# The MLP's seven-product scheme with its token halves exchanged, and VectorE and ScalarE in program order during the output projection

## The chip, the cores and the metric

The kernel runs on one core of one Trainium2 chip. Its time is the device time of one execution in microseconds; of several runs the median is taken. The engines are named as the profile names them: PE (matmul, with PEld for its weight loads), DVE (VectorE), ACT (ScalarE), POOL (GpSimd) and SP (SyncE, which here issues DMAs).

## The reference

One block of a decoder for 512 tokens and 1024 dimensions: a norm, an input projection, two kinds of sparse attention, a gated merge of the two, an output projection with a residual add, and an MLP. The change touches what comes from the output projection on:

```python
    mix = (jax.nn.sigmoid(gate_a) * (o_a @ w_branch_a[l])
           + jax.nn.sigmoid(gate_b) * (o_b @ w_branch_b[l]))
    x = x + mix @ w_out[l]                       # 512x1024 @ 1024x1024
    h = rmsnorm(x, norm_mlp[l])
    x = x + jnp.square(jax.nn.relu(h @ w_mlp_in[l])) @ w_mlp_out[l]   # 1024 -> 4096 -> 1024
return rmsnorm(x, norm_final)
```

## The kernel before

All products are float32 made of three float32r matmuls: a factor is cast to a high part (on ACT), the difference to it is its low part (a subtraction on DVE or POOL), and high*high, high*low and low*high are added up in PSUM.

**Output projection.** The merged branches lie in SBUF as mixh and mixl, 128 dimensions by 512 tokens in 8 chunks, made in the order 4, 5, 6, 7, 0, 1, 2, 3. The result is made in 8 tiles of 128 tokens by 512 dimensions: wo00 to wo03 for the first half of the dimensions, wo10 to wo13 for the second. A tile is 24 matmuls: 16 that go through the chunks with mixh and mixl against wo0hh (the high part of w_out), then 8 with wo0hl. The weights of the second half (wo1r, loaded in 8 pieces, then wo1hh and wo1hl) are split while the first half is running. Behind each tile DVE adds it to the residual x2, ACT makes its sum of squares (sq, with ssq) and, in the first half, a root of the mean (rt); DVE takes the reciprocal (rti) and makes xg, the tile times that preliminary factor and times the norm's weights. PE transposes xg in four matmuls (L1401), placed among the matmuls of the following tile: `TP` says after how many.

**The MLP's first layer** takes its channels in 16 pairs of blocks (2 x 128). A pair is a product of two by two blocks (halves of the dimensions by halves of the tokens, and halves of the dimensions by the two channel blocks), made in seven block products instead of eight, numbered 1 to 7. Each has an operand of x2 (a token half of a dimension half, or a sum or difference of two: `x_sum`, the xt tiles; split by `x_split` into xb, xd or xshh and xshl) and an operand of weights (`w_part`: the sum ws if one is needed, its high part wm on ACT and its low part on POOL, or on DVE for the products of `LOV` from pair 2 on). The loads are wmi, one pair in two tiles. A product is 12 matmuls of 256 tokens into a PSUM tile z. `collect` copies it (ACT) or adds it (DVE) to one or two halves of zt, as `uses` has it. ORDER is the order of the products. Of pair 0 four products belong to the output projection's block of code, with six weight operands made ahead of them (the list `w0`).

**The second layer** (mo) follows in groups of four channel blocks; its weights wmoh and wmol come from wmor, and the result is added to x2 by DVE with the rows' final norm factor r2, which `row_factors` makes from ssq and rt: five small operations on 4 elements a row.

**What sets the order.** A scheduler orders each engine's instructions from the program's, except inside a `manual_schedule`, where the named engines keep program order. Before, such a block covers PE alone, and begins at the transposes in tile wo10; it ends behind the first four products. Tiles come from pools by tag with a fixed number of buffers (`ta` five, `m` two, `q` four, `wr` three): a new tile waits for the last reader of the one whose buffer it takes. DMA loads stand on SP's queue in order.

## Time and profile before

| | us |
|---|---|
| median of 3 runs | 788.96 |
| lowest and highest | 786.49, 788.99 |
| profiled execution, its run's time | 791.72 |
| profiled execution, its span | 789.9 |
| of it: everything before the output projection | 387.1 |
| output projection, to the first product of the MLP | 48.9 |
| MLP's pairs 0 to 3, with two token tiles of the second layer's first group | 58.7 |
| from there to the last group of the second layer | 257.3 |
| last group and final norm | 37.9 |

The stages' bounds are first matmuls in the trace (387.11, 436.02, 494.75, and the last group at about 752). Times inside the profiled execution add up to its span, and not to a median. A row of the timeline has the start, the length, engine, line, operation, what is written and read, shape and count; in brackets the idle time of the engine just before it and what ended it. An engine's instructions overlap by a little, so the pace is the distance of two starts and not the length of one.

### The profile page before, as it was taken

To read this page: it belongs to the slowest core of one execution; us is meant where nothing else is said; L and a number is where in the kernel's file an instruction comes from. 1 tells how busy PE (TensorE), PEld (TensorE's weight loads), DVE (VectorE), ACT (ScalarE), POOL (GpSimd) and SP (SyncE) were. 2 spreads that over 40 slices of the span, in tenths; PEclk is the share of its full clock that TensorE was granted. 3 is DMA by queue.
4 is the path that set the end of the run, shared out by engine and by line. 5 is a ranking of instruction groups with operands and counts; after the bars stand their busy time and mean duration, and the time that the engine had idled before them with its cause. 6 is when DMAs were issued, how large, how long until landed. Compare 5 with 4: busy or idle time off the path is not lost.

```text
span 789.9 us, 12161 instructions
## 1 busy us (share of the span) xinstructions
PE 752.7 (95%) x4267; PEld 645.9 (82%) x4267; DVE 578.7 (73%) x1301; ACT 470.8 (60%) x975; POOL 290.4 (37%) x183
## 2 busy tenths in 40 slices
PE   7999898999999999989999979999999999999996
PEld 4888687777887788867877979888888999999985
DVE  5344678999999966656747999778778696877444
ACT  6533786778667889985344755645454454644234
POOL 3714643232332347763122862312223141414022
PEclk9999999999999999999999999999999999999999
DMA  9454736253344425464630623222314141413002
GB/s 293 112 165 136 202 88 164 80 141 93 94 140 117 153 69 169 140 229 163 237 107 15 225 81 107 80 89 76 130 54 160 54 160 54 161 54 107 1 27 108
DMA packets 87502, 95.55 MB, mean 121 GB/s; under 512 B 8598, under 2 KB 69654, under 8 KB 87408
## 3 DMA queue, kind: packets, MB, share of 16 engines
q1 hardware_dynamic: 83984, 92.97, 36.9%
q0 software_dynamic: 3456, 1.80, 1.2%
q8 instruction: 34, 0.56, 0.3%
q14 instruction: 28, 0.23, 0.1%
HBM read 86.29 MB, written 14.74 MB: 128 GB/s over the span
## 4 chain that ended last, share of the span: by engine, by line
PE 66%; DVE 19%; ACT 6%; DMA 5%; issue 2%; POOL 1%; SPq 0%; DVEq 0%; ACTq 0%; POOLq 0%
PE mo L1551 8%; PE mo L1554 7%; PE mo L1552 7%; PE z L117 6%; PE z L113 6%; PE z L114 6%; PE wo L1438 2%; PE pg L125 2%; PE pg L123 2%; DVE work L667 2%; PE pg L128 2%; DVE ws L1330 2%; DVE m L666 2%; DVE work L648 1%; DMA w1rv<-in_cmp_w_v 1%
## 5 line engine op out<-in xcount | busy, mean ns | idle before, releaser
L1552 PE MATMUL mo<-wmoh,al 128*128 128x512 f32 (+1 forms) x260 | 100.6, 390 | 0.6 <-DVE al L1494 0.6
L1551 PE MATMUL mo<-wmoh,ah 128*128 128x512 f32 (+1 forms) x260 | 100.9, 393 | 0.3 <-ACT ah L1492 0.2
L1503 POOL TENSOR_TENSOR wmol<-wmor,wmoh 128x1024 fp32r<-128x1024 f32 x17 | 49.6, 2921 | 114.1 <-ACT wmoh L1502 114.0
L1334 POOL TENSOR_TENSOR wm<-wmi,wm 128x512 fp32r<-128x512 f32 x32 | 50.1, 1583 | 109.5 <-ACT wm L1333 109.5
L1333 ACT CAST wm<-ws 128x512 fp32r<-128x512 f32 x80 | 49.3, 622 | 49.4 <-PE z L117 25.3
L1555 DVE SCALAR_TENSOR_TENSOR x<-mo,r,x 128x512 f32<-128x512 f32 (+1 forms) x65 | 47.7, 739 | 41.2 <-PE mo L1554 41.0
L1554 PE MATMUL mo<-wmol,ah 128*128 128x512 f32 (+1 forms) x260 | 70.3, 392 | 0.0
L106 POOL TENSOR_TENSOR wg_l<-wr_g,wg_h 128x1024 fp32r<-128x1024 f32 x16 | 38.4, 2401 | 80.2 <-PE pg L128 29.6
L113 PE MATMUL z<-xshh,wm 128*128 128x256 f32 x256 | 64.1, 283 | 2.5 <-DVE zt L1350 2.5
L1350 DVE TENSOR_TENSOR zt<-zt,z 128x256 f32<-128x256 f32 x128 | 48.6, 413 | 23.4 <-ACT zt L1348 16.8
L114 PE MATMUL z<-xshl,wm 128*128 128x256 f32 x256 | 63.9, 282 | 0.0
L1330 DVE TENSOR_TENSOR ws<-wmi 128x512 f32<-128x512 f32 x74 | 62.3, 852 | 1.0 <-POOL wm L1334 0.7
L1348 ACT ACTIVATE zt<-z 128x256 f32<-128x256 f32 x64 | 22.5, 384 | 65.8 <-PE z L117 65.8
L1551 PEld LDWEIGHTS mo<-wmoh,ah 128*128 128x128 f32 x260 | 48.7, 188 | 11.7 <-DVE x L1555 0.6
L1334 DVE TENSOR_TENSOR wm<-ws,wm 128x512 fp32r<-128x512 f32 x70 | 52.3, 763 | 8.2 <-ACT wm L1333 8.2
L1552 PEld LDWEIGHTS mo<-wmoh,al 128*128 128x128 f32 x260 | 48.9, 188 | 11.2 <-DVE al L1494 0.8
L1554 PEld LDWEIGHTS mo<-wmol,ah 128*128 128x128 f32 x260 | 48.6, 188 | 11.0
L1502 ACT CAST wmoh<-wmor 128x1024 fp32r<-128x1024 f32 x32 | 32.1, 1050 | 41.5 <-PE mo L1552 35.1
L123 PE MATMUL pg<-hTh,wg_h 128*128 128x512 f32 x128 | 53.0, 414 | 0.0
L125 PE MATMUL pg<-hTl,wg_h 128*128 128x512 f32 x128 | 52.6, 411 | 0.0
L113 PEld LDWEIGHTS z<-xshh,wm 128*128 128x128 f32 x256 | 48.7, 190 | 2.9 <-issue 1.7
L114 PEld LDWEIGHTS z<-xshl,wm 128*128 128x128 f32 x256 | 48.7, 190 | 0.0
(427 smaller groups left out, 2206.3 us busy)
## 6 DMA issues: line engine op xcount, KB each, us to landing
wmi<-in_w_mlp_in SPq DMA_DIRECT2D x32, 512.0 KB, 4.8
wmor<-in_w_mlp_out SPq DMA_DIRECT2D x32, 512.0 KB, 3.6
wr_g<-in_w_in SPq DMA_DIRECT2D x16, 512.0 KB, 3.8
d_rev<-d_vr SPq DMA_DIRECT2D x8, 640.0 KB, 5.7
x<-in_x SPq DMA_DIRECT2D x8, 512.0 KB, 7.8
d_t<-th SPq DMA_DIRECT2D x16, 256.0 KB, 2.0
stb<-d_rev SPq DMA_DIRECT2D x8, 256.0 KB, 2.8
wr_qa<-in_w_in SPq DMA_DIRECT2D x4, 512.0 KB, 3.6
```

The lines of the kernel that those rows point to most:

```text
L113: PE.matmul(o, wh(k), xh(k), start=start and n == 0, stop=False)
L114: PE.matmul(o, wh(k), xl(k), start=False, stop=False)
L123: PE.matmul(o, wh(k), xh(k), start=k == 0, stop=False)
L125: PE.matmul(o, wh(k), xl(k), start=False, stop=False)
L1330: V.tensor_tensor(t, src, more[0], op=w_blocks[m][2])
L1333: A.copy(w[:, 0], src)
L1334: (V if p > 1 and m in LOV else G).tensor_sub(w[:, 1], src, w[:, 0].bitcast(F32))
L1350: V.tensor_tensor(c, c, o, op=ALU.add if sign > 0 else ALU.subtract)
L1503: (V if ff % 4 in LOO and ff else G).tensor_sub(lo, r, hi.bitcast(F32))
L1551: PE.matmul(o, act[f][0][:, js], wm[f][0][:, cs], start=f == 0, stop=False)
L1552: PE.matmul(o, act[f][1][:, js], wm[f][0][:, cs], start=False, stop=False)
L1554: PE.matmul(o, act[f][0][:, js], wm[f][1][:, cs], start=False, stop=f == FG - 1)
```

## The change

Five edits, all between the start of the output projection and the MLP's first pairs.

1. The token halves change places in the scheme: what the products took from the second half they now take from the first, and the other way round. The blocks of x2 are made in the order (0,0), (0,1), (1,0), (1,1): dimension half, token half. Before, product 2 takes (0,0), 6 the sum (0,0)+(0,1), 4 (1,0)-(0,0), and four need the last block: 5 takes (1,1), 1 (0,0)+(1,1), 7 (1,0)+(1,1), 3 (0,1)-(1,1). After, 2 takes (0,1), 6 (0,0)+(0,1), 1 (0,1)+(1,0), 3 (0,0)-(1,0), 5 (1,0), and two need the last block: 4 takes (1,1)-(0,1), 7 (1,0)+(1,1). `uses` is exchanged to match, `ORDER` is 2, 6, 5, 1, 3, 4, 7 instead of 2, 4, 6, 1, 7, 5, 3, and the six weight operands made ahead are now those of 2, 6, 5, 1, 3, 4.
2. PE, DVE and ACT keep program order in the whole output projection, where before PE alone did in its second half. For this the splits of x2's operands, which were generators stepped through by a list (`GO`), are now two parts: `x_split` makes the high parts and returns a function `lo` for the low parts, called behind the next tile's square.
3. In the second half xg is made ahead of the square. Transposes come after 14 matmuls of the next tile instead of 12, 12 and 10.
4. Low parts of weights: those of pair 1 for products 1, 2, 5, 6, 7 run on DVE instead of POOL. Low parts of x2's operands on POOL: those of 3 and 7 in token tiles 0, 1 and 2, 3, where before those of 7 (tile 2) and 3 (tiles 2 and 3).
5. In `row_factors` POOL makes four of the five operations (the reduction becomes an add of two columns), DVE the reciprocal.

```diff
-    ORDER = (2, 4, 6, 1, 7, 5, 3)
+    ORDER = (2, 6, 5, 1, 3, 4, 7)
-    TP = ((18, 18, 18, 18), (18, 12, 12, 10))
-    XP = ((7, 2), (3, 2), (3, 3))
+    TP = ((18, 18, 18, 18), (18, 14, 14, 14))
+    WP = (0, 0, 1, 1, 1, 1, 1, 1)
+    XP = ((3, 0), (3, 1), (7, 2), (7, 3))
-    uses = {3: ((0, 1, 1), (1, 1, 1)), 5: ((0, 1, 1), (0, 0, -1)), 1: ((0, 0, 1), (1, 1, 1)),
-            2: ((1, 1, -1), (1, 0, 1)), 4: ((0, 0, 1), (1, 0, 1)), 6: ((1, 1, 1),), 7: ((0, 0, 1),)}
+    uses = {3: ((0, 0, 1), (1, 0, 1)), 5: ((0, 0, 1), (0, 1, -1)), 1: ((0, 1, 1), (1, 0, 1)),
+            2: ((1, 0, -1), (1, 1, 1)), 4: ((0, 1, 1), (1, 1, 1)), 6: ((1, 0, 1),), 7: ((0, 1, 1),)}
...
-        (V if p > 1 and m in LOV else G).tensor_sub(w[:, 1], src, w[:, 0].bitcast(F32))
+        (V if p and m in LOV else G).tensor_sub(w[:, 1], src, w[:, 0].bitcast(F32))
...
         if q == (0, 0):
-            gens = [x_split(2, j, t)]
+            ops = []
         elif q == (0, 1):
-            gens = [x_sum(6, j, full(0, 0), t, ALU.add)]
+            ops = [x_sum(6, j, full(0, 0), t, ALU.add), (2, j, t)]
         elif q == (1, 0):
-            gens = [x_sum(4, j, t, full(0, 0), ALU.subtract)]
+            ops = [x_sum(1, j, full(0, 1), t, ALU.add), x_sum(3, j, full(0, 0), t, ALU.subtract), (5, j, t)]
         else:
-            gens = [x_split(5, j, t), x_sum(1, j, full(0, 0), t, ALU.add),
-                    x_sum(7, j, full(1, 0), t, ALU.add), x_sum(3, j, full(0, 1), t, ALU.subtract)]
-        for i in GO if len(gens) > 1 else (0,) * 3:
-            next(gens[i], None)
+            ops = [x_sum(4, j, t, full(0, 1), ALU.subtract), x_sum(7, j, full(1, 0), t, ALU.add)]
+        los = [x_split(*o) for o in ops]
+        return lambda: [f() for f in los]
...
+    ms2.enter_context(tc.manual_schedule(engines={eng.PE, eng.DVE, eng.Activation}))
...
-                    if (half, j) == (1, 0):
-                        ms2.enter_context(tc.manual_schedule(engines={eng.PE}))
-                    x2_transposes(*last)
+                    los = x2_transposes(*last)
...
+            if half:
+                V.scalar_tensor_tensor(xg, x2[j][:, cs], rti[:, j:j + 1], gmlp[:, cs], op0=ALU.mult, op1=ALU.mult)
             A.activation(sq, x2[j][:, cs], AF.Square, accum_out=ssq[:, j, half:half + 1])
             if half == 0:
                 A.activation(rt[:, j:j + 1], ssq[:, j, 0:1], AF.Sqrt, bias=eps_t, scale=1.0 / S)
+            if los:
+                los()
+            if half == 0:
                 V.reciprocal(rti[:, j:j + 1], rt[:, j:j + 1])
-            V.scalar_tensor_tensor(xg, x2[j][:, cs], rti[:, j:j + 1], gmlp[:, cs], op0=ALU.mult, op1=ALU.mult)
+                V.scalar_tensor_tensor(xg, x2[j][:, cs], rti[:, j:j + 1], gmlp[:, cs], op0=ALU.mult, op1=ALU.mult)
-            for _ in range((0, 0, 1, 1, 2, 1, 1, 0)[half * NT + j]):
+            for _ in range(WP[half * NT + j]):
...
-        V.tensor_reduce(r2, ssq, axis=AX.X, op=ALU.add)
-        V.tensor_scalar(r2, r2, 1.0 / DM, EPS, op0=ALU.mult, op1=ALU.add)
+        G.tensor_add(r2, ssq[:, :, 0], ssq[:, :, 1])
+        G.tensor_scalar(r2, r2, 1.0 / DM, EPS, op0=ALU.mult, op1=ALU.add)
         V.reciprocal(r2, r2)
-        V.tensor_mul(rt, rt, rt)
-        V.tensor_mul(r2, r2, rt)
+        G.tensor_mul(rt, rt, rt)
+        G.tensor_mul(r2, r2, rt)
```

What moves on the engines, at three places. In the rows a name with its tile number is written, then what is read (numbers behind an underscore are the buffers').

PE, the end of the first tile of the output projection, before:

```order
L1438 MATMUL wo00_4692<-wo0hh_3955,mixh_4452 128x512
L1438 MATMUL wo01_4724<-wo0hh_3955,mixh_4452 128x512
L1438 MATMUL wo02_4767<-wo0hh_3955,mixh_4452 128x512
L1438 MATMUL wo02_4767<-wo0hh_3955,mixl_4453 128x512
L1438 MATMUL wo02_4767<-wo0hh_3955,mixh_4452 128x512
L1438 MATMUL wo00_4692<-wo0hh_3955,mixl_4453 128x512
L1438 MATMUL wo00_4692<-wo0hh_3955,mixh_4452 128x512
L1438 MATMUL wo01_4724<-wo0hh_3955,mixl_4453 128x512
L1438 MATMUL wo00_4692<-wo0hh_3955,mixl_4453 128x512
L1438 MATMUL wo00_4692<-wo0hl_3956,mixh_4452 128x512 x8
```

and after, the end of wo00 and the start of wo01, and further on in wo01 the transposes of xg00, which stand before the last six of its 24 matmuls:

```order
L1439 MATMUL wo00_4694<-wo0hh_3955,mixh_4452 128x512
L1439 MATMUL wo00_4694<-wo0hh_3955,mixl_4453 128x512
L1439 MATMUL wo00_4694<-wo0hl_3956,mixh_4452 128x512 x8
L1439 MATMUL wo01_4726<-wo0hh_3955,mixh_4452 128x512
L1439 MATMUL wo01_4726<-wo0hh_3955,mixl_4453 128x512
```

```order
L1439 MATMUL wo01_4726<-wo0hh_3955,mixh_4452 128x512
L1439 MATMUL wo01_4726<-wo0hh_3955,mixl_4453 128x512
L1439 MATMUL wo01_4726<-wo0hl_3956,mixh_4452 128x512 x2
L1404 MATMUL xt00_4745<-ident_76,xg00_4720 128x128 x4
L1439 MATMUL wo01_4726<-wo0hl_3956,mixh_4452 128x512 x6
L1439 MATMUL wo02_4765<-wo0hh_3955,mixh_4452 128x512
```

The first three tiles' matmuls, which were taken in turn, are now one tile after the other.

ACT, the splits of wo1r's last pieces and the square of the first tile, before:

```order
L475 CAST wo1hh_4646<-wo1r6_4672 128x512
L475 CAST wo1hh_4646<-wo1r7_4676 128x512
L1333 CAST wm0_4_4857<-wmi01_4681 128x512
L1441 ACTIVATE sq00_4718,ssq_4688<-x2_0_4634 128x512
L1443 ACTIVATE rt_4690<-ssq_4688,small_75 128x1
```

after:

```order
L475 CAST wo1hh_4646<-wo1r6_4672 128x512
L1445 ACTIVATE sq00_4721,ssq_4688<-x2_0_4634 128x512
L475 CAST wo1hh_4646<-wo1r7_4676 128x512
L1447 ACTIVATE rt_4690<-ssq_4688,small_75 128x1
L1412 COPY xf00_4750<-xt00_4745 128x4x128
```

and DVE behind it, where xg00 and so the first transposes come from, before:

```order
L476 TENSOR_TENSOR wo1hl_4647<-wo1r6_4672,wo1hh_4646 128x512
L1439 SCALAR_TENSOR_TENSOR x2_0_4634<-wo00_4692,x2_0_4634 128x512
L1444 RECIPROCAL rti_4691<-rt_4690 128x1
L1439 SCALAR_TENSOR_TENSOR x2_1_4636<-wo01_4724,x2_1_4636 128x512
L1446 SCALAR_TENSOR_TENSOR xg00_4722<-x2_0_4634,rti_4691,gmlp_4632 128x512
L1444 RECIPROCAL rti_4691<-rt_4690 128x1
L1446 SCALAR_TENSOR_TENSOR xg01_4765<-x2_1_4636,rti_4691,gmlp_4632 128x512
```

after:

```order
L1440 SCALAR_TENSOR_TENSOR x2_0_4634<-wo00_4694,x2_0_4634 128x512
L476 TENSOR_TENSOR wo1hl_4647<-wo1r6_4672,wo1hh_4646 128x512
L1451 RECIPROCAL rti_4691<-rt_4690 128x1
L1452 SCALAR_TENSOR_TENSOR xg00_4720<-x2_0_4634,rti_4691,gmlp_4632 128x512
L1440 SCALAR_TENSOR_TENSOR x2_1_4636<-wo01_4726,x2_1_4636 128x512
L1451 RECIPROCAL rti_4691<-rt_4690 128x1
L1452 SCALAR_TENSOR_TENSOR xg01_4759<-x2_1_4636,rti_4691,gmlp_4632 128x512
```

The square of tile 0 (sq00) now stands between the casts of wo1r6 and wo1r7, the root behind the latter; DVE goes on to tile 1 only after xg00.

DVE, from the sums for the last token block (xt13) to the sum of pair 1's product 1 (ws1_1), before:

```order
L1393 TENSOR_TENSOR xt13_5091<-xf00_4748,xt13_5086 128x512
L1393 TENSOR_TENSOR xt73_5093<-xf10_4932,xt13_5086 128x512
L1393 TENSOR_TENSOR xt33_5096<-xf02_4836,xt13_5086 128x512
L1388 TENSOR_TENSOR xshl_4862<-xt13_5091,xshh_4861 128x4x128
L1388 TENSOR_TENSOR xshl_4862<-xt73_5093,xshh_4861 128x4x128
L1388 TENSOR_TENSOR xshl_4862<-xt13_5086,xshh_4861 128x4x128
L1330 TENSOR_TENSOR ws1_2_5212<-wmi10_4684,wmi11_4685 128x512
L1330 TENSOR_TENSOR ws1_6_5250<-wmi10_4684 128x512
L1330 TENSOR_TENSOR ws1_1_5269<-wmi10_4684,wmi11_4685 128x512
```

after, first the rows to the sums of pair 1's product 2:

```order
L1465 RECIPROCAL r2_4689<-r2_4689 128x4
L1396 TENSOR_TENSOR xt43_5097<-xt13_5092,xf02_4832 128x512
L1396 TENSOR_TENSOR xt73_5099<-xf10_4931,xt13_5092 128x512
L1390 TENSOR_TENSOR xshl_4864<-xt43_5097,xshh_4863 128x4x128
L1331 TENSOR_TENSOR ws0_7_5181<-wmi01_4681 128x512
L1331 TENSOR_TENSOR ws1_2_5212<-wmi10_4684,wmi11_4685 128x512
```

and directly behind them, to ws1_1:

```order
L1331 TENSOR_TENSOR ws1_6_5232<-wmi10_4684 128x512
L1351 TENSOR_TENSOR zt01_5143<-zt01_5143,z0_6_5079 128x256
L1351 TENSOR_TENSOR zt00_5142<-zt00_5142,z0_3_5151 128x256
L1351 TENSOR_TENSOR zt00_5142<-zt00_5142,z0_1_5118 128x256
L1351 TENSOR_TENSOR zt01_5143<-zt01_5143,z0_1_5118 128x256
L1351 TENSOR_TENSOR zt00_5142<-zt00_5142,z0_4_5166 128x256
L1351 TENSOR_TENSOR zt01_5143<-zt01_5143,z0_4_5166 128x256
L1335 TENSOR_TENSOR wm1_2_5214<-ws1_2_5212,wm1_2_5214 128x512
L1351 TENSOR_TENSOR zt01_5143<-zt01_5143,z0_3_5151 128x256
L1335 TENSOR_TENSOR wm1_6_5234<-ws1_6_5232,wm1_6_5234 128x512
L1331 TENSOR_TENSOR ws1_5_5251<-wmi10_4684,wmi11_4685 128x512
L1331 TENSOR_TENSOR ws1_1_5271<-wmi10_4684,wmi11_4685 128x512
```

Three sums and three low parts behind the last block are now two and one, the reciprocal of the row factors stands ahead of them, the sum for product 7 of pair 0 (ws0_7) has come in, and the zt adds now stand between pair 1's sums: ws1_1 comes eleven rows behind the sum for its product 6 instead of one, behind two low parts (wm1_2, wm1_6) and seven zt adds.

More of the change, by code (lines that the diff above doesn't have):

```diff
@@ L1300, in block_kernel @@
     PAIRS = DFF // (2 * P)
-    ORDER = (2, 4, 6, 1, 7, 5, 3)
+    ORDER = (2, 6, 5, 1, 3, 4, 7)
     TA = 5
-    GO = (1, 2, 1, 3, 1, 2, 0, 2, 0, 3, 3)
     MF = 2
-    TP = ((18, 18, 18, 18), (18, 12, 12, 10))
-    XP = ((7, 2), (3, 2), (3, 3))
+    TP = ((18, 18, 18, 18), (18, 14, 14, 14))
+    WP = (0, 0, 1, 1, 1, 1, 1, 1)
+    XP = ((3, 0), (3, 1), (7, 2), (7, 3))
     LOV = (1, 2, 5, 6, 7)
@@ L1385, in x_split, with lo @@
             A.copy(h, c)
-        yield
-        for h, l, c in parts:
-            (G if (m, j) in XP else V).tensor_sub(l, c, h.bitcast(F32))
-        yield
+        def lo():
+            for h, l, c in parts:
+                (G if (m, j) in XP else V).tensor_sub(l, c, h.bitcast(F32))
+        return lo
     def x_sum(m, j, a, b, op):
@@ L1393, in x_sum @@
         V.tensor_tensor(t, a, b, op=op)
-        yield
-        yield from x_split(m, j, t)
+        return m, j, t
     def x2_transposes(half, j, xg):
@@ L1410, in x2_transposes @@
         if q == (0, 0):
-            gens = [x_split(2, j, t)]
+            ops = []
         elif q == (0, 1):
-            gens = [x_sum(6, j, full(0, 0), t, ALU.add)]
+            ops = [x_sum(6, j, full(0, 0), t, ALU.add), (2, j, t)]
         elif q == (1, 0):
-            gens = [x_sum(4, j, t, full(0, 0), ALU.subtract)]
+            ops = [x_sum(1, j, full(0, 1), t, ALU.add), x_sum(3, j, full(0, 0), t, ALU.subtract), (5, j, t)]
         else:
-            gens = [x_split(5, j, t), x_sum(1, j, full(0, 0), t, ALU.add),
-                    x_sum(7, j, full(1, 0), t, ALU.add), x_sum(3, j, full(0, 1), t, ALU.subtract)]
-        for i in GO if len(gens) > 1 else (0,) * 3:
-            next(gens[i], None)
+            ops = [x_sum(4, j, t, full(0, 1), ALU.subtract), x_sum(7, j, full(1, 0), t, ALU.add)]
+        los = [x_split(*o) for o in ops]
+        return lambda: [f() for f in los]
     ms2 = ExitStack()
-    last = None
+    ms2.enter_context(tc.manual_schedule(engines={eng.PE, eng.DVE, eng.Activation}))
+    last = los = None
     for half in range(2):
@@ L1434, in block_kernel @@
                 if n == TP[half][j] and last:
-                    if (half, j) == (1, 0):
-                        ms2.enter_context(tc.manual_schedule(engines={eng.PE}))
-                    x2_transposes(*last)
+                    los = x2_transposes(*last)
                 PE.matmul(o, m[:, k, js], w[:, k], start=n == 0, stop=n == len(mm) - 1)
             V.scalar_tensor_tensor(x2[j][:, cs], o, 0.5, x2[j][:, cs], op0=ALU.mult, op1=ALU.add)
+            xg = mp.tile([P, S], F32, tag="ta", bufs=TA, name=f"xg{half}{j}")
+            if half:
+                V.scalar_tensor_tensor(xg, x2[j][:, cs], rti[:, j:j + 1], gmlp[:, cs], op0=ALU.mult, op1=ALU.mult)
             sq = mp.tile([P, S], F32, tag="m", bufs=MB, name=f"sq{half}{j}")
@@ L1443, in block_kernel @@
                 A.activation(rt[:, j:j + 1], ssq[:, j, 0:1], AF.Sqrt, bias=eps_t, scale=1.0 / S)
+            if los:
+                los()
+            if half == 0:
                 V.reciprocal(rti[:, j:j + 1], rt[:, j:j + 1])
-            xg = mp.tile([P, S], F32, tag="ta", bufs=TA, name=f"xg{half}{j}")
-            V.scalar_tensor_tensor(xg, x2[j][:, cs], rti[:, j:j + 1], gmlp[:, cs], op0=ALU.mult, op1=ALU.mult)
+                V.scalar_tensor_tensor(xg, x2[j][:, cs], rti[:, j:j + 1], gmlp[:, cs], op0=ALU.mult, op1=ALU.mult)
             last = (half, j, xg)
-            for _ in range((0, 0, 1, 1, 2, 1, 1, 0)[half * NT + j]):
+            for _ in range(WP[half * NT + j]):
                 w0.append(w_part(0, ORDER[len(w0)], len(w0)))
     o0 = [product(0, ORDER[n], n, w0[n]) for n in range(MF)]
-    x2_transposes(*last)
+    los = x2_transposes(*last)
+    los()
     o0 += [product(0, ORDER[n], n, w0[n]) for n in range(MF, 4)]
```

## The prediction

> **What bounds the kernel now.** I read the page first, then the busy time by stage, then single rows of each stage that the change touches. The page:
>
> ```profile
> span 789.9 us, 12161 instructions
> PE 752.7 (95%) x4267; PEld 645.9 (82%) x4267; DVE 578.7 (73%) x1301; ACT 470.8 (60%) x975; POOL 290.4 (37%) x183
> wmi<-in_w_mlp_in SPq DMA_DIRECT2D x32, 512.0 KB, 4.8
> ```
>
> The matmul engine is busy 752.7 of 789.9 us, so a change that removes no matmul can win at most its idle time. Where that lies, by stage (the columns are the stretch and its length, then busy us of PE, PEld, DVE, ACT and POOL, the granted clock, the DMA share and GB/s):
>
> ```profile
> 387.10:436.00 48.90, 47.69 (x221) 38.47 (x220) 30.46 (x48) 24.45 (x51) 14.28 (x11) 1.00 0.23 71
> 436.00:494.70 58.70, 53.42 (x389) 49.96 (x388) 56.56 (x87) 36.68 (x73) 34.31 (x21) 1.00 0.42 135
> 494.70:752.00 257.30, 257.30 (x1599) 231.10 (x1599) 188.18 (x295) 127.83 (x229) 70.00 (x35) 1.00 0.27 91
> 752.00:789.90 37.90, 31.05 (x145) 25.07 (x143) 17.84 (x31) 14.58 (x32) 11.33 (x7) 0.98 0.19 70
> ```
>
> The first is the output projection, the second the MLP's pairs 0 to 3, the third the rest of them, the fourth the last group and the final norm. In the third PE is busy in every microsecond and stays so: the matmuls are as many, DVE has 69 us to spare and POOL 187. The fourth, like all before 387.10, has the same instructions in the same order in both kernels. So the sum has two stages, 48.90 and 58.70 us; in the second DVE is busy 56.56 of 58.70, so there VectorE paces as much as PE does.
>
> PE's pace and idle times in them (a bracket is idle time before the row and what ended it):
>
> ```profile
> 387.11 0.39 PE L1438 MATMUL wo<-wo0hh,mixh 128*128 128x512 f32 x1
> 389.38 0.61 PE L1438 MATMUL wo<-wo0hh,mixh 128*128 128x512 f32 x2
> 416.34 0.66 PE L1401 MATMUL xt<-ident,xg 128*128 128x128 f32 x4 [1.06 <-DVE xg L1446]
> 418.22 0.39 PE L1438 MATMUL wo<-wo1hh,mixh 128*128 128x512 f32 x1
> 424.15 0.39 PE L1438 MATMUL wo<-wo1hh,mixh 128*128 128x512 f32 x1
> 436.02 0.28 PE L113 MATMUL z<-xb2h,wm 128*128 128x256 f32 x1
> 437.46 0.28 PE L113 MATMUL z<-xshh,wm 128*128 128x256 f32 x1
> 448.41 0.36 PE L113 MATMUL z<-xb2h,wm 128*128 128x256 f32 x1 [0.32 <-DVE zt L1350]
> 464.36 0.36 PE L113 MATMUL z<-xshh,wm 128*128 128x256 f32 x1 [1.55 <-DVE zt L1350]
> 467.41 0.36 PE L113 MATMUL z<-xb2h,wm 128*128 128x256 f32 x1 [1.39 <-ACT zt L1348]
> 470.05 0.39 PE L113 MATMUL z<-xshh,wm 128*128 128x256 f32 x1 [0.98 <-DVE zt L1350]
> 494.75 0.39 PE L1551 MATMUL mo<-wmoh,ah 128*128 128x512 f32 x1
> ```
>
> From 387.11 to 389.38 ten matmuls issue: 0.227 us each, so a tile of 24 takes 5.44; the tile from 418.22 to 424.15 with four transposes in it takes 5.93, so transposes cost 0.49. The output projection is 8 x 5.44 + 7 x 0.49 = 46.95 of PE work in 48.91 us (387.11 to 436.02): 1.95 are lost, 1.06 of it at 416.34. A product of the seven is 12 matmuls in 1.44 (436.02 to 437.46). Up to 494.75 there are 28 products, 48 matmuls of the second layer at 0.23 and one set of transposes: 40.3 + 11.0 + 0.5 = 51.8 of 58.73, so 6.9 are lost, 4.24 of it in the four brackets shown behind 436.02.
>
> **The change, step 1: program order in the projection's first half.** Before, PE takes matmuls of wo00, wo01 and wo02 in turn while chunks 2 and 3 of the mixed branches are still being made. After, wo00 must end before wo01 starts. The chunks' last two operations:
>
> ```profile
> 390.52 1.23 ACT L1281 CAST mixh<-ta 128x512 fp32r<-128x512 f32 x2 [1.42 <-DVE ta L1280]
> 391.62 1.28 DVE L1282 TENSOR_TENSOR mixl<-ta,mixh 128x512 fp32r<-128x512 f32 x2
> ```
>
> PE has 12 matmuls that need neither chunk: until 387.11 + 12 x 0.227 = 389.83. The last low part is there at 391.62 + 1.28 = 392.90; that matmul and eight with wo0hl follow (9 x 0.227 = 2.04), so wo01 starts at 394.95 where unhindered it would at 387.11 + 5.44 = 392.55: **2.4 lost**.
>
> **Step 2: the transposes of xg00, now in wo01.** They stand after 18 of its matmuls, at 394.95 + 4.09 = 399.04. What they wait for, in before's times:
>
> ```profile
> 397.10 0.63 ACT L475 CAST wo1hh<-wo1r 128x512 fp32r<-128x512 f32 x1 [1.95 <-DMA wo1r<-in_w_out]
> 398.22 0.62 ACT L475 CAST wo1hh<-wo1r 128x512 fp32r<-128x512 f32 x1 [0.49 <-DMA wo1r<-in_w_out]
> 398.92 1.29 POOL L476 TENSOR_TENSOR wo1hl<-wo1r,wo1hh 128x512 fp32r<-128x512 f32 x1 [2.40 <-ACT wo1hh L475]
> 404.09 0.63 ACT L1441 ACTIVATE sq<-x 128x512 f32<-128x512 f32 x1
> 404.84 0.30 ACT L1443 ACTIVATE rt<-ssq,small 128x1 f32<-128x1 f32 x1
> 405.17 0.16 DVE L1444 RECIPROCAL rti<-rt 128x1 f32<-128x1 f32 x1 [6.06 <-ACT rt L1443]
> 405.84 0.74 DVE L1446 SCALAR_TENSOR_TENSOR xg<-x,rti,gmlp 128x512 f32<-128x512 f32 x1
> ```
>
> ScalarE, now in program order, has the square of tile 0 behind the cast of wo1r6, which a DMA holds until 397.10: cast to 397.73, square 0.75 (404.09 to 404.84) to 398.45, the cast of wo1r7 0.62 to 399.07, root 0.30, reciprocal 0.16, xg 0.74: 400.25. That is **1.2 late**. But POOL's low part of wo1r7 (1.29) starts just then, at 399.07, and xg00 reads two tiles from SBUF. What such a meeting does:
>
> ```profile
> 421.96 2.55 POOL L1334 TENSOR_TENSOR wm<-ws,wm 128x512 fp32r<-128x512 f32 x2 [8.65 <-ACT wm L1333]
> 423.78 1.28 DVE L1388 TENSOR_TENSOR xshl<-xt,xshh 128x512 fp32r<-128x512 f32 x1 [0.69 <-ACT xshh L1385]
> 444.69 5.50 POOL L1503 TENSOR_TENSOR wmol<-wmor,wmoh 128x1024 fp32r<-128x1024 f32 x2
> 445.03 2.90 DVE L1330 TENSOR_TENSOR ws<-wmi,wmi 128x512 f32<-128x512 f32 x1
> 478.23 1.28 DVE L1334 TENSOR_TENSOR wm<-ws,wm 128x512 fp32r<-128x512 f32 x2
> 479.43 1.07 DVE L1350 TENSOR_TENSOR zt<-zt,z 128x256 f32<-128x256 f32 x3
> ```
>
> Undisturbed, DVE's operation on two 512-wide tiles takes 0.60 of its queue (478.23 to 479.43 for two) and a zt add, which reads one operand from PSUM, 0.33 (three in 1.07). Started beside POOL it takes 1.28 and 2.90, and ends 0.55 after POOL's operation does (POOL 424.51, DVE 425.06). The Trainium skill, "SBUF — State Buffer", section "Who interferes with whom", says that such VectorE and GpSimd instructions exclude each other for the whole of an instruction; those two rows agree; by the rule this step's loss is 1.8, without it 1.2. By the rows xg00 ends at 399.07 + 1.29 + 0.55 = 400.9: **1.8 lost** (low end 1.2, no overlap; high end 2.5, both of POOL's neighbours in the way, another 0.6). The other transposes come 1 us or more after their xg, so the 1.06 at 416.34 goes too: in half 1 xg is made ahead of the square.
>
> Stage sum: 46.95 + 2.4 + 1.8 = 51.2 against 48.91, **+2.3**; the projection ends at 438.3.
>
> **Step 3: the exchanged token halves.** Before, three sums and one plain operand (four splits) wait for the last token block, after it only the sums for products 4 and 7. In before:
>
> ```profile
> 437.81 0.15 DVE L1456 TENSOR_REDUCE r<-ssq 128x4 f32<-128x8 f32 x1
> ...
> 438.76 1.00 DVE L1460 TENSOR_TENSOR r<-r,rt 128x4 f32<-128x4 f32 x1
> 439.69 1.87 DVE L1393 TENSOR_TENSOR xt<-xf,xt 128x512 f32<-128x512 f32 x3
> 441.48 1.88 DVE L1388 TENSOR_TENSOR xshl<-xt,xshh 128x512 fp32r<-128x512 f32 x3
> ```
>
> After: products 2 and 6 to 441.2, eleven matmuls of product 3 to 442.5, the last transposes to 443.0, two sums, a cast (0.62) and one low part on DVE: 445.2 (before: 443.4). Meanwhile PE has products 5 and 1 until 446.0 and then 4: no wait, and 447.4 is reached without loss. Product 7 and the next pair's 2 and 6 carry PE to 447.4 + 3 x 1.44 = 451.8. DVE meanwhile makes seven SBUF operations (the sums of 7, and of pair 1's 2, 6, 5, 1, and two low parts that POOL had before) and seven zt adds: 7 x 0.60 + 7 x 0.33 = 6.5, then a cast, 452.4. That alone is 0.6 late. Beside it POOL has the low part for product 7's last block (1.29), wmol0 (5.50 / 2 = 2.75) and wm0_7 (1.29), 5.3 in all; up to 2.3 of it can lie beside zt adds, so 3.0 are added: 3.6 late at product 1 of pair 1. The low parts of pair 1's products 1 and 3 (the latter on POOL behind wmol1, 2.75 + 1.29) cost an estimated 0.4 and 0.9 more. Lost: 4.9 to 5.0 against 6.9, **-1.9** (bounds: 2.0, nothing of POOL's in the way, so -4.9; and 6.9 or more, nothing won, so 0 or above).
>
> **Step 4: edits I cost at nothing.** The row factors, 437.81 to 439.76 on DVE, become four small POOL operations and one reciprocal on DVE. The reciprocal now waits for POOL, and the sums of the last block are queued behind it; those start when the transposes end at 443.0, and POOL has the sum of squares from about 439.8 (438.3 + an add of 0.69 + a square of 0.75), so some 3 us, less a low part of 1.29 that stands between, hide it. If the cover goes, PE waits for product 4. SP puts the load of wmor1 ahead of pair 3's two, and it waits for the last reader of wmi01, DVE's sum of 7 at about 447; with 4.8 us to land they come by 455, and pair 3 is wanted after 470. The moved token-half signs of the zt copies and adds are as many as before.
>
> **Sum.** 789.9 + 2.3 - 1.9 = 790.3 for the profiled execution. That execution's run took 791.72, of which 1.8 lies around the span, and stands 2.76 above the median of the runs. I put the change on the median: 788.96 + 0.4, **789.4 us**. Between two comparisons about 0.3% (2.4 us) can be told from no change; the forecast is "no change that can be told".
>
> **Rivals.**
> *POOL does not stand in VectorE's way (faster).* If POOL's operations fall beside zt adds and idle time, xg00 costs 1.2 and the MLP's start loses 0.6 + 0.4 + 0.9 = 1.9: (46.95 + 3.6 - 48.91) + (1.9 - 6.9) = 1.6 - 5.0 = -3.4, **785.6**. For it: five low parts of pair 1 leave POOL for DVE. Against it: POOL's chain of 5.3 starts at the same moment as DVE's. Chance 0.2.
>
> *VectorE's new order only moves the waits (slower).* In program order a zt add stands behind sums and low parts that a POOL operation holds, and PE's next product waits for a bank of PSUM that this add must empty. The brackets at 464.36, 467.41 and 470.05 are such waits already, 0.98 to 1.55 each. Were the MLP's start to lose 6.9 again, the sum is +2.3 (**791.3**); one more wmol of 2.75 ahead of product 1 or 3 of pair 1, with half the gain kept, makes it 2.3 - 0.95 + 2.75 = +4.1, **793.1**. It decides once DVE reaches the sum for pair 1's product 1 after 457 (the price at which nothing is won: 455.4 + 1.9). Chance 0.19.
>
> *POOL holds the reciprocal (slower).*
>
> ```profile
> 13.21 2.39 POOL L106 TENSOR_TENSOR wf_l<-wr_f,wf_h 128x1024 fp32r<-128x1024 f32 x1
> ```
>
> POOL has run no tensor-and-scalar operation in before; its first tensor-and-tensor one took 2.39, no more than later ones of that width (2.75 each at 444.69, beside DVE). If the new kind took as long once as POOL's longest entry of this stage, 5.50, from 441.3 to 446.8, the sums that wait from 443.0 come 3.8 late; PE has 0.8 of slack at product 4, so +3.0 on the forecast, **792.4**. It decides from 443.8 on. Chance 0.06, since the row at 13.21 shows no price of a first run. The Trainium skill, "GPSIMD Engine Reference", section 2.1 "Instruction dispatch", gives about 6 us for the first call to a freshly loaded kernel; by it the time would be 792.9, and that row does not bear it out.
>
> *Nothing changes*, as PE is the bound nearly everywhere: that needs both stages' sums near zero, and lies inside my forecast's range.
>
> **How the numbers follow.** Forecast 0.52 (its own range 787.0 to 791.8), POOL not in the way 0.2, waits moved 0.19 (0.13 of it beyond 791.4), reciprocal 0.06, and 0.03, mishaps of both signs. Faster is the first rival and 0.02 of the rest, 0.22; slower 0.13 + 0.06 and 0.06 from the forecast's edge and the rest, 0.25; same what is left, 0.53. The range reaches from the first rival to the second's high end: 785.6 to 793.0, with some 0.15 outside.
>
> **What would show it.** In the profile after: wo01's first matmul at about 395.0; an idle time of PE of 1.2 to 1.9 before the first transposes, put down to xg; no bracket of 1 us before the second half's transposes; the first product at about 438.3; the sums for products 4 and 7 right behind the last transposes, with the reciprocal ahead of them and no idle time of PE before product 4; one bracket of about 3.6 before pair 1's product 1, at about 455; the four brackets of 0.32 to 1.55 gone or smaller; second-layer matmuls at 495.2 where before at 494.75, and from there the same length. A first product before 437 or after 439.5 proves steps 1 and 2 wrong; a loss behind it under 3 or over 7 proves step 3 wrong.

## The result, and the profile after

The changed kernel is slower: 796.49 us (795.59 to 796.96) against 787.96 (786.49 to 788.99), a ratio of 1.0103 with a 95% interval of 1.008 to 1.0126. The forecast was 789.4 with a range of 785.6 to 793.0.

First the page of the changed kernel, then its busy time by stage, with the stages cut at the same events as before (start to end and length, busy us of PE, PEld, DVE, ACT, POOL, granted clock, DMA share, GB/s):

```profile
span 793.8 us, 12180 instructions
PE 752.7 (95%) x4267; PEld 646.0 (81%) x4267; DVE 601.9 (76%) x1301; ACT 471.5 (59%) x975; POOL 284.1 (36%) x183
```

```profile
383.40:435.00 51.60, 47.91 (x222) 38.59 (x221) 32.96 (x47) 24.56 (x53) 16.36 (x14) 1.00 0.18 57
435.00:498.50 63.50, 55.83 (x389) 51.26 (x388) 57.75 (x89) 37.19 (x71) 26.40 (x17) 0.97 0.41 133
498.50:756.00 257.50, 257.50 (x1600) 231.24 (x1599) 206.68 (x295) 130.05 (x229) 69.66 (x36) 1.00 0.28 91
756.00:793.80 37.80, 30.86 (x143) 24.84 (x141) 17.32 (x30) 13.47 (x30) 11.34 (x7) 0.95 0.19 70
```

The projection grew from 48.9 to 51.6 and the MLP's start from 58.7 to 63.5; the two later stages are as long as before. That is +7.6 us from the first matmul of the projection to the end (402.84 to 410.41 by the first and last rows). The spans differ by 3.9 alone because the same instructions ahead of the projection took 387.1 us in the execution profiled before and 383.4 in this one. So stages are compared below, and not spans.

Where PE waited (the last bracket of each row is the idle time ahead of it and what ended it):

```profile
383.41 0.39 PE L1439 MATMUL wo<-wo0hh,mixh 128*128 128x512 f32 x1
387.49 0.50 PE L1439 MATMUL wo<-wo0hh,mixh 128*128 128x512 f32 x1 [1.21 <-ACT mixh L1281]
388.65 0.50 PE L1439 MATMUL wo<-wo0hh,mixl 128*128 128x512 f32 x1 [0.66 <-DVE mixl L1282]
391.43 0.39 PE L1439 MATMUL wo<-wo0hh,mixh 128*128 128x512 f32 x1
397.50 0.65 PE L1404 MATMUL xt<-ident,xg 128*128 128x128 f32 x4 [1.83 <-DVE xg L1452]
447.70 0.39 PE L113 MATMUL z<-xb6h,wm 128*128 128x256 f32 x1 [1.17 <-ACT wm L1334]
449.63 0.74 PE L117 MATMUL z<-xb2h,wm 128*128 128x256 f32 x4 [0.71 <-DVE wm L1335]
452.91 0.38 PE L113 MATMUL z<-xshh,wm 128*128 128x256 f32 x1 [1.13 <-ACT wm L1334]
460.44 0.74 PE L117 MATMUL z<-xdth,wm 128*128 128x256 f32 x4 [1.42 <-POOL wm L1335]
463.99 0.38 PE L113 MATMUL z<-xb6h,wm 128*128 128x256 f32 x1 [0.46 <-DVE zt L1351]
468.03 0.50 PE L1559 MATMUL mo<-wmoh,al 128*128 128x512 f32 x1 [2.36 <-DVE al L1501]
```

The first five rows are the projection: two waits for the mixed chunks and one for xg00, all in its first half, and none in the second. The last six are the MLP's start. The longest, 2.36, ends with the low part of the first activations (al), for the second layer. Behind it the granted clock falls (same columns as the stages):

```profile
465.60:468.00 2.40, 0.07 (x1) 0.00 (x0) 2.40 (x3) 0.00 (x0) 2.40 (x3) 1.00 0.63 207
468.00:469.00 1.00, 0.97 (x4) 0.84 (x5) 1.00 (x4) 0.00 (x1) 1.00 (x1) 0.99 0.57 234
469.00:472.10 3.10, 3.10 (x9) 2.33 (x8) 3.10 (x6) 2.72 (x5) 0.12 (x1) 0.50 0.20 59
```

For 3.1 us the clock is 0.50: PE is "busy" all the time and gets nine matmuls through, at starts 0.43 apart instead of 0.23. What delayed al, and two of the sums before it:

```profile
442.39 1.80 DVE L1331 TENSOR_TENSOR ws<-wmi,wmi 128x512 f32<-128x512 f32 x1
444.11 2.88 DVE L1331 TENSOR_TENSOR ws<-wmi 128x512 f32<-128x512 f32 x1
464.19 2.11 DVE L1335 TENSOR_TENSOR wm<-ws,wm 128x512 fp32r<-128x512 f32 x1
466.23 1.75 DVE L1501 TENSOR_TENSOR al<-zt,ah 128x512 fp32r<-128x512 f32 x1
```

```profile
441.82 1.82 POOL L1390 TENSOR_TENSOR xshl<-xt,xshh 128x512 fp32r<-128x512 f32 x1 [2.42 <-ACT xshh L1386]
443.86 2.58 POOL L1510 TENSOR_TENSOR wmol<-wmor,wmoh 128x1024 fp32r<-128x1024 f32 x1 [0.22 <-ACT wmoh L1509]
463.36 2.39 POOL L1510 TENSOR_TENSOR wmol<-wmor,wmoh 128x1024 fp32r<-128x1024 f32 x1 [2.97 <-ACT wmoh L1509]
465.70 3.42 POOL L1335 TENSOR_TENSOR wm<-wmi,wm 128x512 fp32r<-128x512 f32 x2
```

Each DVE row takes 0.68 undisturbed and here ends about 0.55 behind a POOL operation (444.19 and 443.64; 446.99 and 446.44; 466.30 and 465.75; al at 467.98 and the first of the last row's two at 467.43). ScalarE had made what al reads long before, at 460.14:

```profile
459.50 0.64 ACT L1500 ACTIVATE zt<-zt 128x512 f32<-128x512 f32 x1
```

So al was late by its place in DVE's queue, and the two held operations at the end of that queue, wm and al itself, took 2.5 us more than their 0.68 each.

### The profile page after: what moved, and what is told of

It reads as the page before. It is cut to its first block, busy times and chain, and to the rows that moved or that the text cites. A ratio compares the mean times of both kernels' runs of the same rounds, so it can differ in the third digit from the quotient of the medians.

```text
span 793.8 us, 12180 instructions
## 1 busy us (share of the span) xinstructions
PE 752.7 (95%) x4267; PEld 646.0 (81%) x4267; DVE 601.9 (76%) x1301; ACT 471.5 (59%) x975; POOL 284.1 (36%) x183
## 4 chain that ended last, share of the span: by engine, by line
PE 69%; DVE 20%; ACT 5%; DMA 3%; issue 2%; SPq 0%; POOL 0%; DVEq 0%; ACTq 0%
PE mo L1559 7%; PE mo L1558 7%; PE mo L1561 7%; PE z L113 6%; PE z L117 6%; PE z L114 6%; PE wo L1439 4%; PE pg L125 2%; PE pg L123 2%; DVE work L667 2%; DVE m L666 2%; PE pg L128 2%; DVE work L648 1%; DVE PTs L971 1%; PE oa L991 1%
## 5 line engine op out<-in xcount | busy, mean ns | idle before, releaser
L1335 DVE TENSOR_TENSOR wm<-ws,wm 128x512 fp32r<-128x512 f32 x75 | 68.8, 925 | 13.5 <-ACT wm L1334 13.4
L1331 DVE TENSOR_TENSOR ws<-wmi 128x512 f32<-128x512 f32 x74 | 72.8, 993 | 0.5
L1334 ACT CAST wm<-ws 128x512 fp32r<-128x512 f32 x80 | 48.9, 621 | 36.1 <-DVE ws L1331 23.3
L1558 PEld LDWEIGHTS mo<-wmoh,ah 128*128 128x128 f32 x260 | 49.0, 189 | 11.6 <-DVE x L1562 0.6
L1351 DVE TENSOR_TENSOR zt<-zt,z 128x256 f32<-128x256 f32 x128 | 48.4, 410 | 4.9 <-PE z L117 4.1
L114 PEld LDWEIGHTS z<-xshl,wm 128*128 128x128 f32 x256 | 48.9, 191 | 0.1
L1498 ACT ACTIVATE zt<-zt 128x512 f32<-128x512 f32 x32 | 20.0, 627 | 41.4 <-DVE zt L1351 41.3
```

The lines of the kernel that those rows point to most:

```text
L114: PE.matmul(o, wh(k), xl(k), start=False, stop=False)
L1331: V.tensor_tensor(t, src, more[0], op=w_blocks[m][2])
L1334: A.copy(w[:, 0], src)
L1335: (V if p and m in LOV else G).tensor_sub(w[:, 1], src, w[:, 0].bitcast(F32))
L1351: V.tensor_tensor(c, c, o, op=ALU.add if sign > 0 else ALU.subtract)
L1558: PE.matmul(o, act[f][0][:, js], wm[f][0][:, cs], start=f == 0, stop=False)
```

## The experiments

"C" is the changed kernel, "B" the kernel before. All numbers of stages are from one profiled execution each. How well they repeat: B and e8, whose second stage is alike, have 58.73 and 58.74, C and e2 63.56 and 63.50. "Stretch" is from the first product's first matmul to the second layer's 97th matmul, by which point each kernel has done the same matmuls, 72.45 us at their undisturbed pace (0.119 us for 256 columns, 0.23 for 512). It is split into that, "slow" (pairs of starts 1.6 to 2.05 times the pace apart, the mark of the halved clock) and waits (the rest). Single matmuls behind a wait fall in that range too: up to 1.2 of "slow" stands in kernels whose clock stayed at 1.00 in the stretch (B, e4, e5, e7 to e13). The halved clock itself is in part chance from one execution to the next (last section). "Held" adds up what DVE's operations with two inputs from SBUF took there beyond 0.68 (1.21 for the 1024-wide); in all fifteen executions every operation lengthened by more than 0.05 runs beside a subtraction or other tensor operation of POOL. The ratio is to B's runs of the same job, with its interval.

| kernel | projection | stretch | waits | slow | held | ratio |
|---|---|---|---|---|---|---|
| B | 48.9 | 79.9 | 7.0 | 0.5 | 14.9 | 1 |
| C | 51.6 | 84.8 | 9.8 | 2.5 | 16.6 | 1.0103 (1.008 to 1.0126) |
| e1, C with pair 1's lows on POOL | 53.3 | 85.7 | 9.7 | 3.5 | 20.2 | 1.0104 (1.007 to 1.0137) |
| e2, C with the factors on DVE | 51.1 | 84.7 | 10.0 | 2.2 | 16.5 | 1.0098 (1.0067 to 1.0129) |
| e3, C without program order | 46.9 | 83.5 | 9.0 | 2.1 | 18.1 | 1.0033 (1.0009 to 1.0056) |
| e4, C with two tiles interleaved | 47.0 | 83.5 | 9.9 | 1.2 | 17.6 | 1.001 (0.9978 to 1.0041) |
| e5, e4 with wmol on DVE | 47.0 | 79.5 | 6.1 | 1.0 | 11.6 | 0.9968 (0.9944 to 0.9992) |
| e6, e4 with 7's weights ahead | 47.0 | 81.5 | 6.5 | 2.6 | 19.4 | 0.9981 (0.9957 to 1.0005) |
| e7, B with pair 1's lows on DVE | 48.4 | 77.2 | 4.4 | 0.4 | 12.3 | 0.9959 (0.9941 to 0.9976) |
| e8, B with program order | 52.1 | 79.9 | 7.0 | 0.5 | 15.0 | 1.0039 (1.001 to 1.0068) |
| e9, e5 and e6 together | 47.0 | 78.4 | 5.4 | 0.6 | 12.7 | 0.9966 (0.9945 to 0.9988) |
| e10, e9 with 7's x2 lows on DVE | 47.0 | 78.9 | 5.5 | 0.9 | 12.0 | 0.9963 (0.9942 to 0.9985) |
| e11, e7 with wmol on DVE, xg first | 48.8 | 78.2 | 5.0 | 0.7 | 8.6 | 0.997 (0.9945 to 0.9994) |
| e12, e4, POOL not reading for wmol | 47.0 | 77.6 | 4.4 | 0.8 | 11.2 | 0.9944 (0.9916 to 0.9973) |
| e13, e7 with later transposes | 47.2 | 77.2 | 4.4 | 0.4 | 12.2 | 0.9943 (0.9924 to 0.9961) |

**Undoing one edit of the change.** e1:

```diff
-        (V if p and m in LOV else G).tensor_sub(w[:, 1], src, ...)
+        (V if p > 1 and m in LOV else G).tensor_sub(w[:, 1], src, ...)
```

> The changed kernel with one edit undone: pair 1's low parts of products 1, 2, 5, 6, 7 are made by POOL again. Theory A (the MLP's start got longer by 4.8 us because VectorE has five operations of 0.60 us more there and arrives late at pair 1's low parts and at the low part of the first activations): 2 to 4 us faster than the changed kernel, 792.5 to 794.5, with the idle time of 2.4 before the second layer's matmuls gone. Theory B (the loss comes with the order of products and the exchanged halves, whoever makes the low parts): within 1 us of 796.5.

Theory A fell: nothing is gained, and the stretch is 0.9 longer. DVE has less to do and is held for 3.6 us more. One wait of 4.1 us stands before pair 1's product 1, and the clock behind it falls (rows of e1 by stretch):

```profile
452.00:456.60 4.60, 0.55 (x4) 0.36 (x4) 3.14 (x5) 4.02 (x7) 3.72 (x3) 1.00 0.16 64
456.60:459.00 2.40, 2.39 (x13) 2.40 (x14) 2.40 (x2) 1.83 (x6) 2.40 (x2) 0.63 0.00 0
```

Its projection is 1.7 longer than C's by another 3.4 us at half clock, from 399.2 on.

e2 puts `row_factors` back as it was.

> The changed kernel with the row factors on VectorE again, all five operations. Theory A and B: within 0.8 us of 796.5, since POOL's four operations ended at 439.4, ahead of the last transposes. If the exchange with POOL costs something after all: 1 to 2 us faster.

As expected: the MLP's start is 63.50 instead of 63.56, and the ratio is C's. e3 puts the manual order back to PE alone, from tile wo10 on:

```diff
-    ms2.enter_context(tc.manual_schedule(engines={eng.PE, eng.DVE, eng.Activation}))
...
                 if n == TP[half][j] and last:
+                    if (half, j) == (1, 0):
+                        ms2.enter_context(tc.manual_schedule(engines={eng.PE}))
                     los = x2_transposes(*last)
```

> The changed kernel with the program order undone: PE alone keeps it, from tile wo10 on, as before the change. Theory A: the projection comes back by 2.6 us (48.9 instead of 51.6), the MLP's start stays at 63.5, so 793.9. Theory C (program order of VectorE and ScalarE is also what makes the MLP's start slow): 789 to 791.

The time, 792.55, is near theory A's 793.9, but by other parts: the projection is 46.9, 2.0 shorter than B's 48.9 and all of it PE work, and the MLP's start 62.3, still 3.6 longer than B's. So without program order the change has a gain in the projection (which of its edits brings it, this run does not show; e13 reaches 47.2 without the exchange), and the loss behind it does not need program order.

e4 keeps program order and takes the waits out by hand (all of the transposes in half 0 one tile later; only the core of the edit is shown):

```diff
+            if half == 0 and j == 0:
+                emit(o, js, 0, 12)
+                o1 = ps("ov", "wo01")
+                emit(o1, slice(P, 2 * P), 0, 12)
+                emit(o, js, 12, 24)
+            elif half == 0 and j == 1:
+                emit(o1, js, 12, 24)
```

> The changed kernel, with the first two tiles of the projection interleaved by hand (12 matmuls of wo00, 12 of wo01, the rest of wo00, the rest of wo01) and the transposes of the first half moved one tile later, so that neither chunk 2 nor xg00 is waited for. Theory A: 51.6 becomes 47.3 in the projection, 4.3 less; the MLP's start begins earlier and keeps its length or gets longer by up to 1, so 792.2 to 793.2. If VectorE or a transfer sets the MLP's start and not the end of the projection: 795 or more.

```profile
387.20:434.20 47.00, 47.00 (x221) 38.80 (x221) 31.88 (x47) 24.40 (x53) 16.43 (x14) 1.00 0.20 62
434.20:496.50 62.30, 54.56 (x389) 50.11 (x388) 58.70 (x89) 36.79 (x71) 27.45 (x17) 1.00 0.41 136
```

The projection has PE busy in all of its 47.0 us, so the 4.6 lost there were those three waits. In the second row PE is busy 54.56 of 62.3, and DVE 58.70. Its clock is 1.00 there, and its waits add up to what C's do (9.9 and 9.8), so the 1.25 that it is shorter than C's is the slow clock. The time, 790.77, is below theory A's 792.2 to 793.2.

**One edit of the change on the kernel before.** e8 has program order and nothing else.

```diff
     ms2 = ExitStack()
+    ms2.enter_context(tc.manual_schedule(engines={eng.PE, eng.DVE, eng.Activation}))
...
-                    if (half, j) == (1, 0):
-                        ms2.enter_context(tc.manual_schedule(engines={eng.PE}))
```

> The kernel before with program order of PE, VectorE and ScalarE in the whole projection and nothing else. If program order is the whole cause of the longer projection: 51 to 52 us instead of 48.9 there, and the MLP's start within 1 us of 58.7. If the order also reaches into the MLP's start (its first four products are inside it): that is longer by more than 1.

Both parts held, the first at the edge of its range: the projection is 52.1, with C's three waits in C's places (1.21, 0.65, 1.83), and the MLP's start 58.74.

e7 makes e1's edit the other way round, on B.

> The kernel before with one edit of the change: pair 1's low parts of products 1, 2, 5, 6, 7 on VectorE. Theory D: the MLP's start of 58.7 us gets longer by 2 to 3. Theory L: shorter by 1 to 3, since POOL is busy there for 10 of 10 us and holds VectorE up. As putting them back on POOL in the changed kernel made its start longer by 0.9, theory L is the likelier.

Theory L: 2.7 shorter, with 2.7 less held. So this edit of the change was worth having by itself.

**What holds VectorE.** In e5 the last operation in `out_weights` runs on DVE for the first four blocks:

```diff
-        (V if ff % 4 in LOO and ff else G).tensor_sub(lo, r, hi.bitcast(F32))
+        (V if ff % 4 in LOO or ff < 4 else G).tensor_sub(lo, r, hi.bitcast(F32))
```

> The kernel with the interleaved tiles (projection 47.0, MLP's start 62.3 us), and the low parts of the second layer's first four weight blocks (wmol0, 1, 3; wmol2 is there already) on VectorE instead of POOL. Theory L (POOL's operations hold up VectorE's for their whole length, so 2.4 to 2.9 us of POOL cost VectorE more than the 1.2 that it needs for the same work): the MLP's start gets shorter by 1 to 3 us, 59.3 to 61.3, and the wait of 1.33 for product 6 of pair 1 goes. Theory D (VectorE's own work binds): longer by 1 to 3.6.

4.0 shorter, more than theory L said, with 3.6 us more work on DVE and 6.0 less held. e12 leaves DVE's work alone:

```diff
+        if ff in (0, 1, 3):
+            G.memset(lo.bitcast(F32), 0.0)
+        else:
```

> The kernel with the interleaved tiles; POOL fills wmol0, 1 and 3 with zeros instead of subtracting, so it reads nothing from SBUF there (the low parts of three of the 32 weight blocks of the second layer are left out), and VectorE's work stays what it is in e4_tiles_interleaved. Theory L (VectorE is held up by POOL's reading): the MLP's start of 62.3 us gets shorter by 2.5 to 5, with VectorE's lengthened operations adding up to 5 us less. Theory D (VectorE's own work and its order): within 1 us of 62.3.

POOL in e12, then DVE there, then the same DVE operations in e4:

```profile
442.08 1.81 POOL L1390 TENSOR_TENSOR xshl<-xt,xshh 128x512 fp32r<-128x512 f32 x1 [2.42 <-ACT xshh L1386]
443.83 1.85 POOL L1528 MEMSET wmol<- 128x1024 f32 x2
```

```profile
442.65 1.79 DVE L1331 TENSOR_TENSOR ws<-wmi,wmi 128x512 f32<-128x512 f32 x1
444.37 0.68 DVE L1331 TENSOR_TENSOR ws<-wmi 128x512 f32<-128x512 f32 x1
444.97 2.06 DVE L1351 TENSOR_TENSOR zt<-zt,z 128x256 f32<-128x256 f32 x6
```

```profile
441.65 1.79 DVE L1331 TENSOR_TENSOR ws<-wmi,wmi 128x512 f32<-128x512 f32 x1
443.36 2.88 DVE L1331 TENSOR_TENSOR ws<-wmi 128x512 f32<-128x512 f32 x1
446.17 2.07 DVE L1351 TENSOR_TENSOR zt<-zt,z 128x256 f32<-128x256 f32 x6
```

The first sum, beside a POOL operation that reads SBUF, takes 1.79 in both. The second takes 2.88 beside wmol0 and 0.68 beside a POOL operation that only writes and runs at the same moment. The MLP's start falls from 62.3 to 56.4, 5.9 with DVE's list unchanged (2.5 to 5 were expected), against 4.0 where DVE had to do the work itself. The rest of DVE's held time in e12, 11.2, comes from the other POOL operations. A limit: the fills (0.96) are also shorter than the subtractions (2.4 to 2.9), so POOL itself comes sooner to its later low parts, and the scheduler put some later rows in another order.

**What else lies in the MLP's start.** e6 makes the weights of product 7 ahead, in the projection, and leaves those of product 3 for later (a list of six product numbers, 2, 6, 5, 1, 4, 7, in place of the first six of ORDER).

> The kernel with the interleaved tiles, with the weights of product 7 of pair 0 made ahead in the projection and those of product 3 (a cast and a low part on POOL, no sum) left for later, as it was before the change. Theory O (what moved into the MLP's start, product 7's sum and its low part, and what stands behind them, costs the time): the MLP's start gets shorter by 1 to 2.5 us, 59.8 to 61.3. Theory D with five more low parts on VectorE as the whole cause: shorter by 0.6 at most.

Theory O: 2.0 shorter. But DVE's low part of pair 1's product 2 stands behind three sums and seven zt adds; a wait of 4.1 us for it appeared, with the clock at 0.5 to 0.6 behind it, so "slow" is 2.6.

> The kernel with the interleaved tiles and both edits together: wmol0, 1 and 3 on VectorE and product 7's weights made ahead. If the two gains (4.0 and 2.0 us in the MLP's start) have separate causes they add: 56.3 us from the first product, 784 to 785 in all. If both take away the same thing, POOL's hold on VectorE, the second adds less than 1: 57.5 to 58.5. The wait of 4.1 us for the low part of pair 1's product 2, which came with the weights made ahead, goes under theory L.

In between: the second edit adds 1.1, and that wait shrank to 2.0 and did not go. What stands ahead of it in DVE's queue now are two of the wmol operations, 1.22 each, so part of it is DVE's own work and not POOL's hold.

> As e9_prep_and_wmol, with the low parts of x2's operand for product 7 on VectorE too (two of 0.60, from POOL's two of 1.3 to 1.8). Theory L: the sum of pair 1's product 2, which these held up for 1.2 us, comes sooner, the MLP's start gets shorter by up to 1. Theory D: longer by up to 1.2.

Theory D: 0.5 longer, though 0.7 less is held. DVE's two more operations cost it as much again.

e11 puts three edits on B: e7's, e5's, and xg ahead of sq with 14 for the places of the transposes.

> The kernel before, token halves and order as they were, with three edits: pair 1's low parts on VectorE, wmol0, 1 and 3 on VectorE, and in the projection's second half xg ahead of the square with the transposes after 14 matmuls. Theory L: the projection loses the 1.06 before a set of transposes (47.9), the MLP's start comes to 52 to 55 from 58.7, so 780 to 783. If the exchange of the token halves is needed for that: no better than e9_prep_and_wmol.

Missed twice, with 48.8 in the projection and 57.0 for the MLP's start. The wait ahead of the transposes is still there (1.09, below), as it stands in tile wo10 and is for xg03 of the first half, which these edits don't reach. And with wmol on DVE too the stretch is 0.9 longer than e7's, though held is the least of all, 8.6: it seems that by then DVE's own work counts for more (e11 has the edit of xg as well, so this is not shown alone).

```profile
415.03 0.66 PE L1401 MATMUL xt<-ident,xg 128*128 128x128 f32 x4 [1.09 <-DVE xg L1448]
```

e13 is e7 with `TP = ((18, 18, 18, 18), (23, 12, 12, 10))`, so these transposes stand 1.1 us later.

> The kernel before with two edits: pair 1's low parts on VectorE (as e7_before_lows_on_dve: projection 48.4, MLP's start to the same point 2.7 shorter than before), and the transposes in tile wo10 after 23 of its matmuls instead of 18, 1.1 us later, since the wait of 1.06 stands at that set. If nothing else waits behind it: projection 47.2 to 47.5 and 784.0 to 785.5. If the wait only moves (to the next tile's transposes, or the sums behind): 48.4 and no gain over e7.

```profile
388.10:435.40 47.30, 47.30 (x222) 38.59 (x221) 30.60 (x48) 24.39 (x51) 14.64 (x11) 1.00 0.23 73
435.40:512.60 77.20, 73.98 (x521) 68.77 (x520) 71.55 (x112) 47.97 (x93) 35.75 (x20) 1.00 0.40 131
```

PE is busy in all of the projection, and the wait did not move on. 784.96 against 788.98 us, 0.9943 (0.9924 to 0.9961): two small edits of the kernel before, and it is ahead of both kernels.

## Why the prediction was wrong

**Steps 1 and 2 were right.** (Two roundings in their working change nothing: 397.73 + 0.75 is 398.48 and not 398.45, and 400.9 less 399.04 is 1.9 and not 1.8.) The chunks were to cost 2.4 and cost 2.58 (391.43 - 383.41 - 5.44); xg00 was to cost 1.8 and cost 1.99 (from the last matmul's start ahead of it at 395.29 to 397.50, less 0.227). The hold too: xg00 ended 0.55 behind POOL's low part (395.64 + 1.26 = 396.90, and 397.45).

```profile
395.64 1.26 POOL L476 TENSOR_TENSOR wo1hl<-wo1r,wo1hh 128x512 fp32r<-128x512 f32 x1 [3.06 <-ACT wo1hh L475]
395.99 1.46 DVE L1452 SCALAR_TENSOR_TENSOR xg<-x,rti,gmlp 128x512 f32<-128x512 f32 x1
```

The stage was to be 51.2 and was 51.6, and the second half had no wait, as said. e8 shows that program order is the whole cause and e4 that the three waits are the whole loss.

**Step 3 failed, and it is most of the error.** It was to lose 4.9 to 5.0 and lost 11.8 (63.56 - 51.8). It has two priced terms, and a third was missing. *The wait at pair 1's product 1*, 3.6: PE had lost 4.5 by then (17.94 us from 434.97 to 452.91, for 108 matmuls, 12.96, and one set of transposes, 0.5), though in four pieces, at product 7 (0.4) and at pair 1's products 6 (1.4), 2 and 6 again (1.4) and 1 (1.3). So far the size held roughly, and the reason as well: the sum of product 6 was held by wmol0 for 2.2 us. *What follows*, "an estimated 0.4 and 0.9 more": this is the step that failed. From 452.91 to the second layer's 49th matmul 7.3 us were lost. The two priced places lost 0.7 (products 1 and 5) and 1.7 (product 3), 2.4 instead of 1.3. The wait at product 3 is POOL's own queue, its low part behind wmol1, as I had said:

```profile
455.84 2.88 POOL L1510 TENSOR_TENSOR wmol<-wmor,wmoh 128x1024 fp32r<-128x1024 f32 x1
458.66 1.73 POOL L1335 TENSOR_TENSOR wm<-wmi,wm 128x512 fp32r<-128x512 f32 x1
```

The rest, 4.8, had no term at all: 0.7 for a zt add ahead of pair 2's product 6, 2.6 for al, and *the clock*, 1.5 behind that wait (e4, without it, is 1.25 shorter). I followed DVE's chain to one product and took the old waits behind it as gone. They stand in before at 464 to 470; in after others stand in their place, at 464 for a zt add and at 468 for al, which was queued behind operations that POOL holds.

The sign of the step rested on fewer sums behind the last token block. That part happened, with no wait before product 4; but e1, with pair 1's low parts on POOL as in B, is 5.7 longer than B in that stretch, at 5.3 more held and 3.0 more slow clock. My reading is that what the exchange saved at the front it gave back by where DVE and POOL then met. Low parts (e1), row factors (e2) and program order (e3, e8) are each ruled out as the cause of this loss. e6 finds one part of the cause, the weights of product 7, which had been made ahead and now were made there (2.0). That the low parts of pair 1 went to DVE, which I counted as DVE's burden, helped (e7, 2.7). How the rest divides between the exchange itself and the order that the scheduler then chose was not separated: no run has the exchange with before's order of products.

**Step 4 was right.** POOL was done with the factors' first half at 437.87 and DVE's reciprocal at 438.08, ahead of the last transposes at 439.2; e2 puts no price on it, and no wait of PE in C's MLP start ended with a load. The first tensor-and-scalar operation on POOL in the profiled execution took 0.50, so the rival with a price for a first run did not come about:

```profile
437.37 0.50 POOL L1464 TENSOR_SCALAR r<-r 128x4 f32<-128x4 f32 x1
437.90 0.18 DVE L1465 RECIPROCAL r<-r 128x4 f32<-128x4 f32 x1
```

The Trainium skill, "GPSIMD Engine Reference", section 2.1 "Instruction dispatch", gives about 6 us for the first call to a freshly loaded kernel; the row has 0.50, and whether it was such a call no run here shows.

**The rivals.** The second one came true in kind (waits moved, not removed) and was priced at 791.3 to 793.1. It was short by 3.4 to 5.2: it let the start lose 6.9 again, and it lost 11.8, of which 1.5 are the clock. The first, POOL not in the way, did not come about by itself; taking three of POOL's readings out by hand (e12) was worth 5.9 in e4's MLP start.

**The base** added a little. The execution that I took for the sum had a stage ahead of the change 3.7 longer than the one after; the median of five runs of B is 787.96 and not 788.96.

## What to carry to other kernels

Where two engines exclude each other on SBUF, count for each of VectorE's operations the POOL operation beside it, over the whole stretch up to where the orders meet again; a chain followed to its first late product leaves out what queues behind it. Moving work from POOL to VectorE can pay although VectorE is the busier (in e5 3.6 us of work against 6.0 of hold), until VectorE's own work is the larger part. Fixed order on an engine is safe only where every operand is early: interleave two tiles, or move the consumer a tile later, when the first operands come from another stage.
